# A 2048-wide hybrid diffusion layer on one core: both early z pieces of a modulation step placed behind all four conditioning batches of the next step

## The chip, the cores and the metric

One core of one Trainium2 chip. The metric is the time on the device in microseconds (us) of one execution; the kernel before takes 2322.63 us (median of three runs). PE is the matrix engine, ACT the scalar engine, DVE the vector engine, POOL the GpSimd engine, SP the engine whose queue issues the weight loads here.

## The reference

One layer of a diffusion backbone for 128 context tokens and 256 latent tokens (384 columns in all), in float32. Only its opening matters here: a conditioning vector gives a shift and a scale for every one of the 2048 channels, the normalised tokens are modulated with them, and the result is multiplied by the wide input projection.

```python
mod = (jax.nn.silu(cond) @ w_ada + b_ada)[:, None, :]
sh1, sc1, g1, sh2, sc2, g2 = jnp.split(mod, N_MOD, axis=-1)
h = rmsnorm(x, norm_mix_pre) * (1 + sc1) + sh1
z = h @ w_in + b_in
```

The three mixer branches, the output projection and the feed-forward part follow; the change does not touch them.

## The kernel before, in words

All weights pass through one list, `stream`, of pieces. Each piece has a load, for most a split, and a use. `run_stream` walks the list; SP issues the loads in the order of the list, as far ahead as there are buffers: 8 buffers `eraw` of 1 MB for the conditioning batches, 4 buffers `raw` of at most 512 KB for all other weights. A load whose buffer is still in use holds up the loads behind it. At most 8 loads are under way at once, since each takes one of eight semaphores in turn.

Float32 products are made from three matmuls (`mm3`, lines 177 to 179) on a high and a low half. So an ordinary weight piece is split first: ACT writes the high half `whi` (line 168), DVE the low half `wlo` (line 169). The split of a piece is issued two matmul pieces ahead of its use. A conditioning batch is not split (`whole`).

The first 150 us work on the scale `S1` and the shift `H1` in eight modulation steps, g = 0 to 7. Step g has four **conditioning batches** ada(g, 0) to ada(g, 3) of 1 MB each (line 393, 4 matmuls of 128x512 with 32 weight columns; the trace counts each of them twice). When the fourth is through, `ada_rows` copies the sums to the tile `row` (ACT, line 401), `ada_cols` turns them into columns with 4 very small matmuls (PE, line 410; "the turn" below), and `ada_mod` computes `S1` and `H1` of two channel tiles (DVE, lines 417 to 419) and then the modulated inputs `hx` of channel tiles 2g and 2g+1: DVE line 366, ACT lines 370, 371 and 374, DVE line 378.

With these two `hx` tiles, seven column tiles of z get two of their sixteen contributions at once, from two **early z pieces**: z(g, 0) with four column tiles (512 KB, 24 matmuls of 128x384) and z(g, 1) with three (384 KB, 18 matmuls). z(0) to z(6) stand in the loop over g, among the batches of the next step; z(7) comes later. Behind the loop stand two pieces of a further column tile, `TY`, with 8 and 6 contributions.

The functions of a piece's `after` run behind the use of the next piece, and one waiting background function of each of three queues behind that:

```python
pc.use(*his.pop(j))          # line 258
...
for f in pend:
    f()                      # ada_rows of the piece before: copy, queue ada_cols
pend = list(pc.after)        # line 265
for b in bgq:
    if b:
        b.popleft()()        # ada_cols at once, ada_mod one piece later
```

So what the list holds just behind ada(g, 3) decides where PE meets the turn, and what it holds behind that decides where `ada_mod` stands on DVE and ACT. Each engine works through its instructions in order.

In the list before, step g (from 1 on) reads ada(g, 0), ada(g, 1), ada(g, 2), z(g-1, 0), ada(g, 3), z(g-1, 1). The copy of `row` is issued behind z(g-1, 1), the turn right behind it, `ada_mod` behind ada(g+1, 0).

## Time and profile before

| | |
|---|---|
| median of three runs | 2322.63 us (2322.43 to 2324.74) |
| the profiled execution | 2323.49 us |
| its span, first to last instruction | 2321.7 us |
| PE busy | 2265.5 us, 98% |
| DVE busy | 1426.9 us, 61% |
| ACT busy | 881.0 us, 38% |
| mean granted PE clock | 0.992 |
| bytes read from HBM | 382.71 MB |

In the views below a row of the timeline has the start and the length of a run of equal instructions, their engine, line and tiles, and in brackets the idle time before them with what ended it. A row of a table of windows gives, for the stretch at its start, its length, the busy time of PE, PE's weight loads (PEld), DVE, ACT and POOL with their instructions, the granted PE clock (1.00 is full), the busy share of the DMA engines and the GB/s they moved.

### The profile page before, as it was taken

To read this page: it belongs to the slowest core of one execution; us is meant where nothing else is said; L and a number is where in the kernel's file an instruction comes from. 1 tells how busy PE (TensorE), PEld (TensorE's weight loads), DVE (VectorE), ACT (ScalarE), POOL (GpSimd) and SP (SyncE) were. 2 spreads that over 40 slices of the span, in tenths; PEclk is the share of its full clock that TensorE was granted. 3 is DMA by queue.
4 is the path that set the end of the run, shared out by engine and by line. 5 is a ranking of instruction groups with operands and counts; after the bars stand their busy time and mean duration, and the time that the engine had idled before them with its cause. 6 is when DMAs were issued, how large, how long until landed. Compare 5 with 4: busy or idle time off the path is not lost.

```text
span 2321.7 us, 31781 instructions
## 1 busy us (share of the span) xinstructions
PE 2265.5 (98%) x12597; PEld 2150.1 (93%) x12597; DVE 1426.9 (61%) x2230; ACT 881.0 (38%) x1362; POOL 31.7 (1%) x72
## 2 busy tenths in 40 slices
PE   6899999999999999999999999999999999999997
PEld 3679999999999999999989999999999999888886
DVE  3247777656788888878556577776444445444444
ACT  3243333444323323324356533333333334334333
POOL 0000000000000000000000000000000000000000
PEclk9999999999999999999999999999999999999999
DMA  9825333234666666768533355554343333344343
GB/s 398 350 97 148 105 117 120 96 120 154 200 227 224 223 222 228 234 197 289 183 97 121 130 189 181 188 185 162 127 140 124 128 123 124 132 130 145 127 131 105
DMA packets 104869, 390.05 MB, mean 168 GB/s; under 512 B 12112, under 2 KB 12256, under 8 KB 100624
## 3 DMA queue, kind: packets, MB, share of 16 engines
q1 hardware_dynamic: 99504, 371.76, 47.5%
q0 software_dynamic: 4064, 14.36, 2.0%
q8 instruction: 98, 1.61, 0.3%
q10 hardware_dynamic: 1152, 1.90, 0.2%
q14 instruction: 51, 0.42, 0.1%
HBM read 382.71 MB, written 5.27 MB: 167 GB/s over the span
## 4 chain that ended last, share of the span: by engine, by line
PE 92%; DVE 1%; ACT 0%; issue 0%; DVEq 0%; ACTq 0%
PE ps L179 23%; PE ps L177 23%; PE ps L178 23%; PE ps L1490 5%; PE ps L1491 5%; PE ps L1489 5%; PE ps L877 1%; PE ps L878 1%; PE ps L876 1%; PE ps L973 1%; PE ps L968 1%; PE ps L912 0%; DVE wlo L169 0%; PE ps L921 0%; PE ps L1013 0%; PE ps L1033 0%
## 5 line engine op out<-in xcount | busy, mean ns | idle before, releaser
L169 DVE TENSOR_TENSOR wlo<-raw,whi 128x1024 fp32r<-128x1024 f32 (+3 forms) x521 | 622.0, 1197 | 725.5 <-ACT whi L168 725.0
L177 PE MATMUL ps<-hx,whi 128*128 128x384 f32 (+1 forms) x3024 | 1028.2, 340 | 19.1 <-ACT whi L168 13.4
L179 PE MATMUL ps<-hx,wlo 128*128 128x384 f32 (+1 forms) x3024 | 1022.9, 338 | 4.4 <-DVE wlo L169 4.4
L178 PE MATMUL ps<-hx,whi 128*128 128x384 f32 (+1 forms) x3024 | 1022.0, 338 | 0.3 <-DVE hx L169 0.2
L168 ACT ACTIVATE whi<-raw 128x1024 fp32r<-128x1024 f32 (+3 forms) x521 | 540.0, 1038 | 1234.2 <-PE ps L178 741.9
L177 PEld LDWEIGHTS ps<-hx,whi 128*128 128x128 f32 x3024 | 572.5, 189 | 33.2 <-ACT whi L168 19.6
L179 PEld LDWEIGHTS ps<-hx,wlo 128*128 128x128 f32 x3024 | 572.4, 189 | 7.0 <-DVE wlo L169 7.0
L178 PEld LDWEIGHTS ps<-hx,whi 128*128 128x128 f32 x3024 | 572.5, 189 | 1.9 <-DVE hx L378 0.7
L1154 DVE SCALAR_TENSOR_TENSOR cb<-raw,cb 128x1024 f32<-128x1024 f32 x256 | 313.0, 1223 | 10.0 <-DMA raw<-w_ada 4.0
L1490 PE MATMUL ps<-whi,hx 128*128 128x512 f32 x528 | 205.5, 389 | 0.8 <-DVE hx L169 0.8
L1489 PE MATMUL ps<-whi,hx 128*128 128x512 f32 x528 | 205.5, 389 | 0.0
L1491 PE MATMUL ps<-wlo,hx 128*128 128x512 f32 x528 | 205.4, 389 | 0.0
L1490 PEld LDWEIGHTS ps<-whi,hx 128*128 128x128 f32 x528 | 99.1, 188 | 21.8 <-DVE hx L169 1.1
L1489 PEld LDWEIGHTS ps<-whi,hx 128*128 128x128 f32 x528 | 99.1, 188 | 20.8 <-ACT hx L168 0.4
L1491 PEld LDWEIGHTS ps<-wlo,hx 128*128 128x128 f32 x528 | 99.1, 188 | 20.5
L691 DVE SCALAR_TENSOR_TENSOR cacc<-cbuf,vec,cacc 128x444 f32<-128x444 f32 x116 | 78.7, 678 | 2.8
L1381 DVE SCALAR_TENSOR_TENSOR t<-t,vec,t 128x192 f32<-128x192 f32 (+1 forms) x176 | 63.7, 383 | 16.0 <-ACT t L1372 12.8
L876 PE MATMUL ps<-whi,hx 128*128 128x256 f32 x192 | 56.5, 294 | 0.0
L393 PE MATMUL ps<-eraw,cs 128*32 128x512 f32 x256 | 37.3, 697 | 17.4 <-DMA eraw<-w_ada 16.7
L877 PE MATMUL ps<-whi,hx 128*128 128x256 f32 x192 | 54.3, 283 | 0.0
L878 PE MATMUL ps<-wlo,hx 128*128 128x256 f32 x192 | 54.3, 283 | 0.0
L169 DVE TENSOR_TENSOR hx<-f,hx 128x384 fp32r<-128x384 f32 x88 | 48.3, 550 | 0.0
(283 smaller groups left out, 1430.0 us busy)
## 6 DMA issues: line engine op xcount, KB each, us to landing
raw<-w_up SPq DMA_DIRECT2D x164, 512.0 KB, 3.7
raw<-w_in SPq DMA_DIRECT2D x163, 512.0 KB, 3.8
raw<-w_ada SPq DMA_DIRECT2D x128, 512.0 KB, 4.4
raw<-w_down SPq DMA_DIRECT2D x88, 512.0 KB, 3.3
eraw<-w_ada SPq DMA_DIRECT2D x32, 1024.0 KB, 14.1
raw<-w_out SPq DMA_DIRECT2D x32, 512.0 KB, 4.5
raw<-w_v SPq DMA_DIRECT2D x16, 512.0 KB, 4.0
raw<-w_br SPq DMA_DIRECT2D x16, 512.0 KB, 5.0
```

The source lines that it names most:

```text
L168: act.activation(hi, src, AF.Copy)
L169: dve.tensor_sub(lo, src, hi.bitcast(F32))
L177: pe.matmul(out, wh, x, start=first, stop=False, skip_group_check=True)
L178: pe.matmul(out, wh, xl, start=False, stop=False, skip_group_check=True)
L179: pe.matmul(out, wl, x, start=False, stop=last, skip_group_check=True)
L691: dve.scalar_tensor_tensor(a, b[:, j : j + CPOS], w, a, ALU.mult, ALU.add)
L876: pe.matmul(outs[t], xh, hi[:, a], start=k == 0 and t != 1, stop=False, skip_group_check=True)
L877: pe.matmul(outs[t], xl, hi[:, a], start=False, stop=False, skip_group_check=True)
L1154: dve.scalar_tensor_tensor(MX["junk"], raw, 1.0, MX["cb"][c][half], ALU.mult, ALU.mult, accum_out=MODR[:, m, n, c, half : half + 1])
L1489: pe.matmul(ps, xh, hi[:, w], start=first, stop=False, skip_group_check=True)
L1490: pe.matmul(ps, xl, hi[:, w], start=False, stop=False, skip_group_check=True)
L1491: pe.matmul(ps, xh, lo[:, w], start=False, stop=last, skip_group_check=True)
```

## The change

Both early z pieces leave their places among the batches and go behind the fourth one. Step g now reads ada(g, 0), ada(g, 1), ada(g, 2), ada(g, 3), z(g-1, 0), z(g-1, 1). The same instructions are issued, as many as before; loads, splits and matmuls follow the list in its new order.

```diff
             stream.append(Piece(i["w_ada1"][g, :, 4 * q : 4 * q + 4], (4, 512), ada_use(g, q), early=True, whole=True,
                                 after=[ada_rows(g)] if q == 3 else None,
                                 onload=load_all_x if g == 0 and q == 0 else None))
-            if q > 1 and g:
-                stream.append(early_piece(g - 1, q - 2))
+        if g:
+            stream.append(early_piece(g - 1, 0))
+            stream.append(early_piece(g - 1, 1))
     stream.append(part_piece(TY, 7, 0, 8))
     stream.append(part_piece(TY, 7, 8, 14))
```

PE, the end of z(0, 0) in step 1 and what follows it, before (L177 to L179 are z, L393 a conditioning batch, L410 the turn):

```order
L179 MATMUL ps_106<-hx_255,wlo_233 128x384
L393 MATMUL ps_214<-eraw_134,cs 32x512 x4
L177 MATMUL ps_107<-hx_251,whi_267 128x384
L178 MATMUL ps_107<-hx_251,whi_267 128x384
L179 MATMUL ps_107<-hx_251,wlo_268 128x384
```

The same place in the change:

```order
L179 MATMUL ps_106<-hx_251,wlo_256 128x384
L410 MATMUL ps_103<-pair,row_303 128x2 x4
L177 MATMUL ps_107<-hx_247,whi_265 128x384
L178 MATMUL ps_107<-hx_247,whi_265 128x384
L179 MATMUL ps_107<-hx_247,wlo_266 128x384
```

The fourth batch is gone from between the two z pieces, and the turn of step 1 stands there instead.

PE, from the end of z(0, 1) to the first matmuls of z(1, 0), before:

```order
L179 MATMUL ps_109<-hx_255,wlo_268 128x384
L410 MATMUL ps_103<-pair,row_321 128x2 x4
L393 MATMUL ps_327<-eraw_143,cs 32x512 x4
L393 MATMUL ps_327<-eraw_160,cs 32x512 x4
L393 MATMUL ps_327<-eraw_178,cs 32x512 x4
L177 MATMUL ps_103<-hx_343,whi_351 128x384
```

And in the change:

```order
L179 MATMUL ps_109<-hx_251,wlo_266 128x384
L393 MATMUL ps_344<-eraw_143,cs 32x512 x4
L393 MATMUL ps_344<-eraw_160,cs 32x512 x4
L393 MATMUL ps_344<-eraw_178,cs 32x512 x4
L393 MATMUL ps_344<-eraw_196,cs 32x512 x4
L177 MATMUL ps_103<-hx_336,whi_357 128x384
```

Between the turn and z(1, 0) there were three batches; now there are z(0, 1) and four batches.

DVE, the opening, from the reciprocal of the token scale on, before (S and H are `S1` and `H1`):

```order
L346 RECIPROCAL r_226<-t_224 128x384
L169 TENSOR_TENSOR wlo_233<-raw_132,whi_232 128x1024
L417 SCALAR_TENSOR_TENSOR S_76<-ps_103,vec 128x4
L418 TENSOR_TENSOR S_76<-S_76,vec 128x4
L419 TENSOR_TENSOR H_77<-ps_103,vec 128x4
L366 TENSOR_TENSOR t_245<-x_94,r_226 128x384
L366 TENSOR_TENSOR t_247<-x_94,r_226 128x384
L378 TENSOR_TENSOR hx_251<-t_245,hx_251 128x384
L378 TENSOR_TENSOR hx_255<-t_247,hx_255 128x384
L169 TENSOR_TENSOR wlo_268<-raw_136,whi_267 128x768
```

And in the change:

```order
L346 RECIPROCAL r_226<-t_224 128x384
L417 SCALAR_TENSOR_TENSOR S_76<-ps_103,vec 128x4
L418 TENSOR_TENSOR S_76<-S_76,vec 128x4
L419 TENSOR_TENSOR H_77<-ps_103,vec 128x4
L366 TENSOR_TENSOR t_241<-x_94,r_226 128x384
L366 TENSOR_TENSOR t_243<-x_94,r_226 128x384
L378 TENSOR_TENSOR hx_247<-t_241,hx_247 128x384
L378 TENSOR_TENSOR hx_251<-t_243,hx_251 128x384
L169 TENSOR_TENSOR wlo_256<-raw_134,whi_255 128x1024
L169 TENSOR_TENSOR wlo_266<-raw_136,whi_265 128x768
```

The split of z(0, 0) now stands behind the modulation of step 0; before it stood ahead of it. ACT's order moves in the same way there. From step 1 on, DVE and ACT keep their order before and after: `ada_mod`, then the splits of z(g, 0) and z(g, 1).

## The prediction

> **What bounds the kernel now.** I read the page first, then a table of windows over the opening and the rest, then the timelines of PE, ACT and DVE over one modulation step.

> ```profile
> span 2321.7 us, 31781 instructions
> PE 2265.5 (98%) x12597; PEld 2150.1 (93%) x12597; DVE 1426.9 (61%) x2230; ACT 881.0 (38%) x1362; POOL 31.7 (1%) x72
> 52.83:69.67 16.84, 13.97 (x82) 10.44 (x82) 4.53 (x10) 5.18 (x10) 0.00 (x0) 0.90 1.01 414
> 69.67:86.61 16.94, 14.08 (x83) 10.54 (x83) 4.55 (x10) 5.19 (x10) 0.00 (x0) 0.90 0.97 378
> 86.61:103.61 17.00, 14.13 (x82) 10.61 (x83) 4.53 (x10) 5.18 (x10) 0.00 (x0) 0.90 0.79 302
> 103.61:120.61 17.00, 14.13 (x83) 10.60 (x83) 4.54 (x10) 5.19 (x10) 0.00 (x0) 0.90 0.62 246
> 120.61:137.61 17.00, 14.14 (x83) 10.61 (x83) 4.53 (x10) 5.18 (x10) 0.49 (x1) 0.90 0.15 54
> 137.61:149.53 11.92, 11.28 (x59) 9.87 (x59) 4.16 (x4) 3.85 (x5) 2.91 (x6) 0.86 0.44 145
> 150.00:2322.00 2172.00, 2152.72 (x11980) 2072.62 (x11978) 1381.59 (x2146) 830.48 (x1275) 25.78 (x57) 1.00 0.48 158
> ```

> PE is busy 98% of the span, and behind 150 us it is busy for 2152.72 of 2172.00 us. What moves the start of that stretch moves the end of the kernel. The changed code lies ahead of it. There every step, from the first matmul of one z(g, 0) to that of the next, takes 16.84 to 17.00 us, whether the loads run at 414 GB/s or at 54 GB/s: the step does not wait for memory. PE is busy 14.1 us of the 17.0, with a clock of 0.90. So two things are lost in each step: idle time and clock.

> One step on PE (x8 and x24 are one and three conditioning batches):

> ```profile
> 59.53 1.06 PE L393 MATMUL ps<-eraw,cs 128*32 128x512 f32 x8
> 60.53 0.45 PE L177 MATMUL ps<-hx,whi 128*128 128x384 f32 x1
> ...
> 63.78 0.95 PE L410 MATMUL ps<-pair,row 128*128 128x2 f32 x8
> 64.66 2.78 PE L393 MATMUL ps<-eraw,cs 128*32 128x512 f32 x24
> 69.67 0.45 PE L177 MATMUL ps<-hx,whi 128*128 128x384 f32 x1 [2.23 <-ACT whi L168]
> ...
> 70.93 0.69 PE L179 MATMUL ps<-hx,wlo 128*128 128x384 f32 x1 [0.64 <-DVE wlo L169]
> ```

> A batch alone takes 1.00 us from start to start (59.53 to 60.53), z(g, 1) 3.25 us for 18 matmuls (60.53 to 63.78), the turn 0.88, three batches 2.78. Then PE stands 2.23 us for `whi`, and 0.64 us for `wlo` two matmuls later.

> What it waits for starts with the turn, on DVE and ACT (DVE's rows first):

> ```profile
> 64.77 0.16 DVE L417 SCALAR_TENSOR_TENSOR S<-ps,vec 128x4 f32<-128x4 f32 x1 [9.87 <-PE ps L410]
> ...
> 65.12 1.01 DVE L366 TENSOR_TENSOR t<-x,r 128x384 f32<-128x384 f32 x2
> 65.70 0.49 ACT L370 ACTIVATE t<-t,H,S 128x128 f32<-128x128 f32 x1 [4.44 <-DVE t L366]
> ...
> 68.58 1.77 ACT L168 ACTIVATE whi<-raw 128x1024 fp32r<-128x1024 f32 x2
> PE ps L177 <- ACT whi L168: 13.4, 6, 2.2
> PE ps L179 <- DVE wlo L169: 3.8, 6, 0.6
> ```

> The turn ends at 64.66. DVE makes `S1` at 64.77, the products at 65.12; ACT makes the two `hx` from 65.70 to 68.58, and only then splits z(g, 0). From the end of the turn to the first matmul it is 69.67 - 64.66 = 5.01 us, to the first use of `wlo` 70.93 - 64.66 = 6.27 us. Three batches cover 2.78 us of this. The two waits come six times, 13.4 and 3.8 us in total.

> The clock is lost for the same reason:

> ```profile
> 84.40:87.90 3.50, 0.65 (x3) 0.33 (x3) 2.24 (x4) 2.86 (x5) 0.00 (x0) 1.00 0.95 386
> 87.90:91.30 3.40, 3.40 (x11) 3.40 (x12) 0.78 (x1) 0.00 (x0) 0.00 (x0) 0.51 1.01 426
> ...
> 98.10:101.40 3.30, 3.28 (x30) 1.16 (x29) 1.52 (x6) 1.73 (x4) 0.00 (x0) 1.00 0.73 226
> 101.40:104.90 3.50, 0.65 (x3) 0.33 (x3) 2.24 (x4) 2.86 (x5) 0.00 (x0) 1.00 0.94 393
> 104.90:108.30 3.40, 3.40 (x11) 3.40 (x12) 0.78 (x1) 0.00 (x0) 0.00 (x0) 0.51 1.00 422
> ```

> In the stretch that holds the waits (84.40 to 87.90) PE is busy 0.65 us of 3.50; in the 3.40 us behind it the granted clock is 0.51, and full again after that. The same again at 101.40. The cold stretch does 1.67 us of work less than a warm one (3.40 x 0.49). [...]

> **The change part by part.** No instruction is added or removed. Three things move.

> *The turn goes ahead of z(g, 1), and the fourth batch ahead of the next z.* The chain of 5.01 us (6.27 for `wlo`) then runs beside z(g, 1), 3.25 us, and four batches, 2.78 + 0.93 = 3.71: 6.96 us in all. The first matmul has 1.9 us to spare. The first `wlo` use, some 0.3 us later, has 1.0. Both waits go. The copy of `row` that the turn needs runs on ACT beside z(g, 0), which takes 24/18 x 3.25 = 4.33 us, so the turn does not wait. With no stretch of low PE activity I expect the clock to stay full: the window 98.10 to 101.40 is nearly all batches, and the one behind it has 1.00, so batches count as activity; the turn alone is 0.88 us.

> A step is then 4.33 (z, first piece) + 0.88 + 3.25 + 3.71 = 12.17 us. In the trace z(1, 0) to z(6, 0) are five steps, 16.84 + 16.94 + 3 x 17.00 = 84.78 us by the windows above. Five new ones are 60.85. **Gain 23.9 us.**

> *The tail.* From the start of z(6, 0) to the first `TY` matmul the trace has 11.92 us, with a batch, a `wlo` wait and a cold stretch in it. Now z(6, 0), the turn and z(6, 1): 4.33 + 0.88 + 3.25 = 8.46. **Gain 3.5 us.** The last `hx` pair has z(6, 1) and both `TY` pieces as cover, more than before.

> *The opening.* DVE (three rows) and PE (the last) there:

> ```profile
> 29.32 2.55 DVE L346 RECIPROCAL r<-t 128x384 f32<-128x384 f32 x1 [12.12 <-ACT t L344]
> 32.33 1.23 DVE L169 TENSOR_TENSOR wlo<-raw,whi 128x1024 fp32r<-128x1024 f32 x1 [0.46 <-ACT whi L168]
> 33.47 0.15 DVE L417 SCALAR_TENSOR_TENSOR S<-ps,vec 128x4 f32<-128x4 f32 x1
> 36.05 0.45 PE L177 MATMUL ps<-hx,whi 128*128 128x384 f32 x1 [2.45 <-ACT hx L374]
> ```

> Before, `wlo` of z(0, 0) went ahead of `S1`. Now `S1` starts at 29.32 + 2.55 = 31.87. The chain of the other steps from there (69.67 - 64.77 = 4.90, 70.93 - 64.77 = 6.16) puts the first z matmul at 36.8 and the first `wlo` use at 38.0. Before it was 36.05 without a `wlo` wait: about 1.0 us later now. Against that stand the 2.23 us wait of z(1, 0), which goes, and the batches, now 3.71 behind z(0, 1) for 1.00 + 2.78: z(1, 0) starts 2.3 - 1.0 = 1.3 us earlier. The clock is cold here and could stay so one window longer (1.7 us), or catch up 0.6. **Gain 1.3 us, between -0.4 and 1.9.**

> *SP's queue.* Loads follow the list, so each step's two z loads go behind its fourth batch. A step loads 4 batches and 512 + 384 KB, 5.11 MB:

> ```profile
> 0.00:15.00 15.00, 0.00 (x0) 0.00 (x0) 6.85 (x15) 8.69 (x18) 2.52 (x8) 1.00 0.89 342
> 15.00:75.00 60.00, 49.25 (x247) 29.13 (x248) 18.06 (x32) 17.64 (x30) 0.00 (x0) 0.91 1.01 417
> 75.00:90.00 15.00, 12.14 (x76) 8.61 (x76) 4.54 (x9) 5.18 (x9) 0.00 (x0) 0.93 0.96 374
> eraw<-w_ada SPq DMA_DIRECT2D x32, 1024.0 KB, 14.1
> SPq L205 <- PE ps L393: 44.3, 17, 6.4
> ```

> At the 417 GB/s of 15 to 75 us this is 12.26 us, just over PE's 12.17. So after the change PE and the loads go at about the same pace, and the lead decides. Up to ada(7, 3) the queue brings 3.46 MB of inputs (2048 x 384 tokens and a 128 x 615 vector tile in float32), 32 x 1.049 MB and six pairs of z, 42.5 MB. By 15 us 5.13 MB are there (342 GB/s), the rest takes 37.4 / 0.417 = 89.7 us: ada(7, 3) lands at 104.7. PE reaches it at z(6, 0) less 0.9 us. By my times z(1, 0) starts near 51.5, z(6, 0) near 112.4, so the load is 6.8 us ahead. The first lead, ada(2, 3) landed at 43.4 for a use at 50.6, is 7.2. The loads' buffers come free soon enough: ada(5, 3) is used near 88, and ada(7, 0) has to be under way by about 95. The later fall in rate is no limit of memory: 302 GB/s x 17.00 us is 5.13 MB, exactly one step, at the pace at which PE frees buffers (SP's 44.3 us of waits for L393). I cost the loads at nothing; their cover is this lead.

> Sum: 23.9 + 3.5 + 1.3 = 28.7 us. The profiled execution took 2323.49 us for a span of 2321.7, which lies 0.86 above the median. I put the gain against the median: 2322.63 - 28.7 = **2293.9 us**. Bounds of this case: with the opening at its ends and 0.1 us of hand-over per step either way, 2290 to 2297.

> **The rivals.**

> *The cold stretch stays.* If these short gaps are not what cools the clock, it is something else in the step, the batches with their 32 columns or the turn, and these stay. Then each of six z(g, 0) keeps its 1.67 us, 10 us in all: 2304. Against it: every cold stretch here follows a window with 0.65 us of work, and windows full of batches are followed by a full clock. [...]

> *The loads do not keep their pace.* At the 374 GB/s of 75 to 90 us instead of 417, ada(7, 3) lands at 15 + 37.4 / 0.374 = 115 us, 3.6 us too late: 2297.5. A rate near this would come if a buffer were freed late in every step. Against it: SP has 8 loads under way and the batches are used 7 us behind their landing.

> *Slower.* The z pieces now need the whole 5.11 MB of a step ahead of them, and everything behind the loop waits for z(6). If the loads fell to the 246 GB/s of 103.61 to 120.61 from the beginning, ada(7, 3) would land at 15 + 37.4 / 0.246 = 167 us, `TY` would start at 167 + 0.9 + 8.5 = 176.4 instead of 149.53, and the time would be 2349.5. The point from which this decides is a landing at 140, that is 299 GB/s. The 417 GB/s of the opening speak against it.

> *The gain is given back later*, since the `raw` loads of the stretch behind 150 us have to come 29 us earlier: 2322. Against it: 54 GB/s at 120 to 137 us show an empty queue, four `raw` buffers ahead.

> **How the numbers follow.** My forecast has 0.74, the cold stretch 0.12, the slower loads 0.08, given back 0.03, slower 0.03. The first alone spans 2290 to 2297. The range of 8 in 10 goes to 2304.5, as far as the cold stretch, and to 2289.5 below: PE could do a step in a little less, but not below its matmuls. A measurement of this kernel can tell about 0.2% (4.6 us) from no change. Faster: 0.94; same: 0.03; slower: 0.03.

> **What would show it.** In the profile of the changed kernel the waits of L177 for `whi` and of L179 for `wlo` ahead of 120 us are down to the opening's; the PE clock between 45 and 120 us is 1.00; the first matmuls of z(g, 0) are 12.2 us apart; `TY` starts near 121 us; the loads run at over 400 GB/s up to 105 us; the stretch behind it is as long as before, some 2172 us. I am wrong if PE waits for `eraw` behind 45 us (the lead was too small), if the clock still shows 0.5 once in a step, or if the stretch behind `TY` has grown.

## The result, and the profile after

The changed kernel takes 2294.22 us (median of four runs, 2293.20 to 2294.96) against 2322.95 us before: the ratio is 0.9871, with a 95% interval of 0.986 to 0.9883. That is 28.7 us less. A second set of runs of the same kernel gave 2293.71 us and 0.9868 (0.9854 to 0.9883).

The same table of windows as for before, on the changed kernel: five steps from z(1, 0) to z(6, 0), the tail up to the first `TY` matmul, and the rest.

```profile
52.17:64.14 11.97, 11.97 (x87) 9.09 (x83) 4.54 (x10) 5.20 (x9) 0.00 (x0) 1.00 1.01 413
...
76.11:88.08 11.97, 11.97 (x87) 9.09 (x83) 4.54 (x10) 5.20 (x9) 0.00 (x0) 1.00 1.01 415
...
100.04:112.01 11.97, 11.97 (x87) 9.09 (x83) 4.54 (x10) 5.97 (x10) 0.49 (x1) 1.00 0.83 336
112.01:120.23 8.22, 8.22 (x54) 8.22 (x51) 3.70 (x8) 2.83 (x6) 2.91 (x6) 1.00 0.57 189
120.23:2293.20 2172.97, 2153.97 (x11983) 2073.89 (x11981) 1380.47 (x2141) 830.30 (x1274) 25.77 (x57) 1.00 0.48 158
```

A step takes 11.97 us instead of 17.00, PE is busy for all of it, and the clock is 1.00 instead of 0.90. Loads run at 413 to 419 GB/s up to 100 us. What follows `TY` is as long as before, 2173 us.

The timeline of PE in the changed kernel, from the first z matmul to that of the next step:

```profile
36.85 0.69 PE L177 MATMUL ps<-hx,whi 128*128 128x384 f32 x1 [2.38 <-ACT whi L168]
...
38.11 0.69 PE L179 MATMUL ps<-hx,wlo 128*128 128x384 f32 x1 [0.25 <-DVE wlo L169]
...
43.40 0.36 PE L177 MATMUL ps<-hx,whi 128*128 128x384 f32 x1
...
44.48 0.95 PE L410 MATMUL ps<-pair,row 128*128 128x2 f32 x8
45.30 0.42 PE L177 MATMUL ps<-hx,whi 128*128 128x384 f32 x1
...
48.59 3.64 PE L393 MATMUL ps<-eraw,cs 128*32 128x512 f32 x32
52.17 0.44 PE L177 MATMUL ps<-hx,whi 128*128 128x384 f32 x1
```

Who PE waited for between 30 and 140 us (us in total, times, longest):

```profile
PE ps L177 <- ACT whi L168: 2.4, 1, 2.4
PE ps L179 <- DVE wlo L169: 0.2, 1, 0.2
```

The turn stands between z(0, 0) and z(0, 1), four batches run in 3.64 us, and z(1, 0) starts with no idle time before it. The waits for `whi` and `wlo`, 13.4 and 3.8 us before, are 2.4 and 0.2 us, both in the opening.

### The profile page after: what moved, and what is told of

Read it like the earlier page. It is cut to its first block, busy times and chain, and to the rows that moved or that the text cites. A ratio compares the mean times of both kernels' runs of the same rounds, so it can differ in the third digit from the quotient of the medians.

```text
span 2293.2 us, 31786 instructions
## 1 busy us (share of the span) xinstructions
PE 2253.0 (98%) x12597; PEld 2143.6 (93%) x12597; DVE 1426.8 (62%) x2230; ACT 880.8 (38%) x1362; POOL 31.7 (1%) x72
## 4 chain that ended last, share of the span: by engine, by line
PE 97%; DVE 1%; DMA 1%; ACT 1%; issue 0%; ACTq 0%; DVEq 0%
PE ps L177 24%; PE ps L179 24%; PE ps L178 24%; PE ps L1491 5%; PE ps L1490 5%; PE ps L1492 5%; PE ps L393 1%; PE ps L878 1%; PE ps L879 1%; PE ps L877 1%; DMA eraw<-w_ada 1%; PE ps L974 1%; PE ps L969 1%; PE ps L913 0%; DVE wlo L169 0%; DMA vec<-vec 0%
## 5 line engine op out<-in xcount | busy, mean ns | idle before, releaser
L169 DVE TENSOR_TENSOR wlo<-raw,whi 128x1024 fp32r<-128x1024 f32 (+3 forms) x521 | 622.2, 1197 | 726.9 <-ACT whi L168 724.7
L177 PE MATMUL ps<-hx,whi 128*128 128x384 f32 (+1 forms) x3024 | 1024.8, 339 | 5.6 <-ACT hx L1294 3.2
L179 PE MATMUL ps<-hx,wlo 128*128 128x384 f32 (+1 forms) x3024 | 1019.1, 337 | 0.8 <-DVE wlo L169 0.8
L168 ACT ACTIVATE whi<-raw 128x1024 fp32r<-128x1024 f32 (+3 forms) x521 | 540.0, 1038 | 1231.8 <-PE ps L178 748.2
L177 PEld LDWEIGHTS ps<-hx,whi 128*128 128x128 f32 x3024 | 570.4, 189 | 12.3 <-issue 5.0
L179 PEld LDWEIGHTS ps<-hx,wlo 128*128 128x128 f32 x3024 | 570.1, 189 | 2.0 <-DVE wlo L169 2.0
L393 PE MATMUL ps<-eraw,cs 128*32 128x512 f32 x256 | 34.7, 675 | 18.6 <-DMA eraw<-w_ada 18.6
L169 DVE TENSOR_TENSOR hx<-f,hx 128x384 fp32r<-128x384 f32 x88 | 48.3, 550 | 0.0
## 6 DMA issues: line engine op xcount, KB each, us to landing
eraw<-w_ada SPq DMA_DIRECT2D x32, 1024.0 KB, 17.1
```

What stands on the lines that cost most here:

```text
L168: act.activation(hi, src, AF.Copy)
L169: dve.tensor_sub(lo, src, hi.bitcast(F32))
L177: pe.matmul(out, wh, x, start=first, stop=False, skip_group_check=True)
L179: pe.matmul(out, wl, x, start=False, stop=last, skip_group_check=True)
```

## The experiments

My theory: the chain behind the turn (S1, products, hx, split) set the step; the change covers it with z(g, 1) and one more batch, which takes the idle time away and with it the cold clock behind it. Rivals: the four batches in one run and the new order of loads bring the gain; the batches themselves cool the clock; the loads are the near bound.

**Only the turn moved.** The list stays as before; copy and turn are issued inside the use of ada(g, 3).

```diff
 # in ada_use, behind the four matmuls
+            if q == 3 and g:
+                ada_rows(g)()
+                bgq[1].pop()()
 # the batch in the loop
-                                after=[ada_rows(g)] if q == 3 else None,
+                                after=[ada_rows(g)] if q == 3 and g == 0 else None,
```

> The list of before (loads, batches and z pieces in their old order); only the copy of row and the turn are issued right behind ada(g, 3), ahead of z(g-1, 1), from step 1 on. My theory, the chain behind the turn sets the step: z(g-1, 1) and three batches, 3.25 + 2.78 = 6.03 us, cover the 5.01 us to the first matmul, so the waits for whi and wlo go and the clock stays at 1.00; instead PE waits some 0.85 us per step for the copy of row. Step 4.33 + 1.00 + 0.85 + 0.88 + 3.25 + 2.78 = 13.1 us, time about 2300.6 (2298 to 2304). Rival A, what gains is the four batches in one run and the loads in the new order: this kernel keeps most of the 17.0 us step, over 2313. Rival B, batches or the turn cool the clock: the waits go, but a clock of about 0.5 for 3.4 us stays in each step, about 2311.

Measured: 2302.57 us against 2323.78 beside it, ratio 0.991 (0.9895 to 0.9924). PE's waits from 30 to 150 us in this kernel:

```profile
PE ps L413 <- ACT row L404: 5.0, 7, 0.7
PE ps L177 <- ACT hx L374: 2.4, 1, 2.4
```

Two turns in its timeline of PE (L413 is the turn there):

```profile
57.67 1.05 PE L413 MATMUL ps<-pair,row 128*128 128x2 f32 x8 [0.72 <-ACT row L404]
...
70.75 1.05 PE L413 MATMUL ps<-pair,row 128*128 128x2 f32 x8 [0.72 <-ACT row L404]
```

The waits for the split are gone, the new one for the copy is 0.72 us, a step is 70.75 - 57.67 = 13.08 us (13.1 expected) and the clock from 45 to 120 us is 1.00. So 21 of the 29 us come from the turn's place alone, with loads and batches in their old order. Rivals A and B fall.

**Only the turn left behind.** The list of the change, with the copy and the turn behind z(g-1, 1).

```diff
-                                after=[ada_rows(g)] if q == 3 else None,
+                                after=[ada_rows(g)] if q == 3 and g == 0 else None,
 ...
-            stream.append(early_piece(g - 1, 0))
+            stream.append(early_piece(g - 1, 0, after=[ada_rows(g)]))
```

> The list of the change; only the copy of row and the turn are issued one piece later, behind z(g-1, 1) as before. My theory: four batches cover 3.71 of the 5.01 us, so PE waits 1.3 us for whi and about 0.6 for wlo in each of six steps, 11.6 us in all: 2306 if the clock stays full with about 1.5 us of work in a window of 3.4, 2316 if that still halves it. Rival A, the order of loads and batches alone brings the gain: 2294 to 2296.

Measured: 2309.24 us, ratio 0.9936 (0.9921 to 0.9951), 15 us more than the change. One step's two waits in its timeline of PE:

```profile
65.92 0.44 PE L177 MATMUL ps<-hx,whi 128*128 128x384 f32 x1 [1.37 <-ACT whi L168]
...
67.17 0.45 PE L179 MATMUL ps<-hx,wlo 128*128 128x384 f32 x1 [0.64 <-DVE wlo L169]
```

A table of windows of 3.41 us, on the grid on which the one cold stretch of these steps begins and ends (the first three around the step above, the last two around the next):

```profile
61.94:65.35 3.41, 2.61 (x28) 0.52 (x16) 1.39 (x3) 3.34 (x7) 0.00 (x0) 1.00 1.02 416
65.35:68.76 3.41, 2.20 (x11) 1.88 (x12) 2.25 (x3) 1.73 (x3) 0.00 (x0) 1.00 1.00 411
68.76:72.17 3.41, 3.41 (x22) 3.41 (x21) 0.00 (x0) 0.00 (x0) 0.00 (x0) 1.00 1.04 420
79.00:82.41 3.41, 1.67 (x8) 1.35 (x9) 2.65 (x3) 2.27 (x4) 0.00 (x0) 1.00 0.98 399
82.41:85.82 3.41, 3.41 (x13) 3.41 (x12) 0.00 (x0) 0.00 (x0) 0.00 (x0) 0.50 1.04 425
```

Both steps have the same waits, 1.37 and 0.64 us (1.36 in the second). Waits of 1.3 and 0.6 us were expected. The time lies between the two given, 2306 with a full and 2316 with a halved clock: the profiled execution has one cold stretch in six steps. In the first step shown the waits fall into two windows with 2.61 and 2.20 us of work, and the clock stays full. In the second step they leave one window with 1.67 us of work, and the clock behind it is 0.50. In the sixth step the same waits leave one window with 1.90 us of work, and the clock behind it stays full:

```profile
123.40:126.82 3.42, 1.90 (x9) 1.58 (x10) 3.03 (x4) 2.51 (x3) 2.51 (x6) 1.00 0.25 41
126.82:130.23 3.41, 3.41 (x22) 3.41 (x21) 0.67 (x1) 0.74 (x1) 0.00 (x0) 1.00 0.94 320
```

Of these four windows only the one with the least work, 1.67 us, was followed by half clock. In the kernel before the clock changes on such a grid, too: its half-clock stretches in the steps begin at 53.80, 70.87, 87.93, 105.00, 122.07 and 139.13 us, 17.07 us apart, which is five times 3.41. The first three in its table of windows:

```profile
53.80:57.21 3.41, 3.12 (x10) 3.13 (x11) 1.10 (x2) 0.00 (x0) 0.00 (x0) 0.50 1.03 416
...
70.87:74.28 3.41, 3.35 (x10) 3.35 (x11) 0.87 (x2) 0.00 (x0) 0.00 (x0) 0.50 1.02 422
...
87.93:91.35 3.42, 3.42 (x11) 3.42 (x12) 0.75 (x1) 0.00 (x0) 0.00 (x0) 0.50 1.01 426
```

Its step of 17.00 us is almost five windows long, so the gap meets nearly the same place of the grid in every step.

**The gap filled with useless work.** The kernel before, with 20 small matmuls behind the third batch of steps 2 to 7.

```diff
+            if q == 2 and g > 1:
+                for n in range(20):
+                    pe.matmul(acc["z", EARLY[1 + n % 6]][:, NT:512], hx[0].hi[:, :P], hx[0].lo[:, :P], start=False,
+                              stop=False, skip_group_check=True)
```

> The kernel before, with 20 small matmuls of 128x128 added behind the third batch of each step from 2 on, in the gap in which PE waits for whi; their sums go into columns that nobody reads. They change no wait, only PE's activity in the gap. My theory, the gap cools the clock: the clock behind it stays at 1.00, z(g, 0) is 1.67 us shorter in six steps, time 2322.9 - 10 = 2313 (2311 to 2316). [...]

Measured: 2316.49 us, ratio 0.9967 (0.9956 to 0.9979), 7.3 us less than the 2323.78 of before beside it and 0.5 above my range. One step in its timeline of PE (L397 is the small matmuls):

```profile
64.08 2.78 PE L393 MATMUL ps<-eraw,cs 128*32 128x512 f32 x24
66.79 2.45 PE L397 MATMUL ps<-hx 128*128 128x128 f32 x20
69.09 0.44 PE L177 MATMUL ps<-hx,whi 128*128 128x384 f32 x1
...
70.35 0.45 PE L179 MATMUL ps<-hx,wlo 128*128 128x384 f32 x1 [0.64 <-DVE wlo L169]
```

The window that follows this gap, in its table of windows:

```profile
69.40:72.80 3.40, 2.76 (x16) 2.45 (x15) 1.76 (x2) 0.38 (x1) 0.00 (x0) 1.00 1.04 424
```

The small matmuls fill the gap up to 69.09, 5.01 us behind the end of the turn at 64.08, as before; no wait has become shorter but `whi`'s, which is now work. The clock behind is 1.00, and the step 15.4 us (turns at 63.20 and 78.64) for 17.0. In all six steps of this execution the clock behind the gap is full, 1.00 for 0.50 in the kernel before. So the gap was what cooled the clock: six steps shortened by some 1.5 us are 9 us. Of these 0.8 were lost in the opening, whose turn of step 1 came at 47.78 us for 46.94 before. By the last turn 8.4 us are gained (140.36 for 148.72), but the whole span is only 6.9 us shorter. Far behind the changed steps, at 1181 us, the clock is half for 10.2 us, where the kernel before has 6.8 us of it at 1190 us; 3.4 us more at half clock take back about 1.7 us.

**Four buffers for batches instead of eight**, once in the change and once in the kernel before (`ERAW` 8 to 4).

> The change with 4 instead of 8 buffers for batches: the load of ada(g+1, q) can then only start when ada(g, q) is used, so the lead of some 7 us that I named as the cover of the loads is taken away. My theory of the lead: four batches freed within 3.6 us need 10.1 us to load and some 2 us to start, the two z loads stand behind them, so z(g, 0) comes up to 1.2 us late: step 12.0 to 13.2 us, time 2294 to 2302, likeliest 2298, with PE waits for whi, wlo or eraw in each step. Rival, the loads are the near bound of the step: each step goes to 15 us or more, over 2312.

> The kernel before with 4 instead of 8 buffers for batches. My theory: its 17.0 us step is set by the chain behind the turn and needs 5.11 MB in 17.0 us, 301 GB/s, so the lost lead costs it little: 2322 to 2327, against some 9 us for the change with 4 buffers. Rival, lead matters as much to the old order: over 2330.

Measured: the change 2303.56 us (2299.41 to 2305.23), ratio 0.9916 (0.9899 to 0.9933); the kernel before 2324.79 us, ratio 1.0002 (0.9992 to 1.0011). PE's waits from 30 to 150 us with four buffers in the change:

```profile
PE ps L177 <- ACT whi L168: 5.7, 4, 2.5
PE ps L179 <- DVE wlo L169: 3.2, 5, 0.6
```

ACT's wait for loads there, from 40 to 122 us:

```profile
ACT whi L168 <- DMA raw<-w_in: 12.3, 7, 3.2
```

The lead does matter to the change (about 10 us) and not to the old order. My likeliest value, 2298, was too low by 5.6, and the median lies above my range for this run; what comes late is not a batch but the `raw` tile of a z piece, for which ACT waits. The 2 us put down for the start of a load were my estimate; in the kernel before, 512 KB that are under way alone land 3.2 us after their issue at 151.09 us, and at 417 GB/s their bytes take 1.26 of these. In the old order with four buffers, as with the turn left behind, the same waits do not halve the clock every time. Two of its steps, from turn to turn, with the same waits of 2.23 and 0.65 us, and below them, for each, the clock's window that holds the waits and the one behind it:

```profile
82.21:97.63 15.42, 12.54 (x84) 9.02 (x84) 4.54 (x9) 5.19 (x9) 0.00 (x0) 1.00 0.86 330
65.22:82.21 16.99, 14.11 (x84) 10.59 (x84) 4.54 (x9) 5.19 (x9) 0.00 (x0) 0.90 0.81 303
...
87.20:90.61 3.41, 1.87 (x9) 1.55 (x10) 2.58 (x3) 1.58 (x2) 0.00 (x0) 1.00 1.01 425
90.61:94.03 3.42, 3.42 (x25) 2.67 (x23) 0.00 (x0) 0.00 (x0) 0.00 (x0) 1.00 0.99 414
...
70.14:73.55 3.41, 1.79 (x9) 1.48 (x10) 2.65 (x3) 1.65 (x2) 0.00 (x0) 1.00 0.99 375
73.55:76.96 3.41, 3.41 (x12) 3.41 (x11) 0.00 (x0) 0.00 (x0) 0.00 (x0) 0.50 0.97 387
```

The second step is cold for a fifth of its time and takes 16.99 us, the first stays warm and takes 15.42. A window with 1.87 us of work left the clock full, one with 1.79 us was followed by half clock.

**A shorter opening.** The change, with the token norm's end one piece earlier; and the same with one full matmul more behind ada(1, 3).

```diff
-    for c in range(4):
-        bgq[0].append(lambda c=c: rms1_part(c))
+    bgq[0].append(lambda: (rms1_part(0), rms1_part(1)))
+    bgq[0].append(lambda: rms1_part(2))
+    bgq[0].append(lambda: rms1_part(3))
     bgq[0].append(rms1_end)
 # second kernel, in ada_use
+            if q == 3 and g == 1:
+                pe.matmul(acc["z", EARLY[1]][:, :NT], ones, R["ss1"], start=True, stop=True, skip_group_check=True)
```

> The change itself once more, as the measure for the two kernels beside it. Every theory: 2294 (2293 to 2295), 0.987 of before.

> The change, with two of the four parts of the sum of squares issued behind the first batch, so that the end of the token norm (one matmul, root, reciprocal) is issued behind ada(0, 3) and not behind ada(1, 0). In the profile of the change S1 of step 0 waits for the reciprocal, which ends at 31.9 us; PE sits idle between the batches from 15 to 25 us. My theory: what is left to gain lies in the opening, on the chain norm, S1, hx, whi, first z matmul at 36.85. The reciprocal ends near 29.4, the turn at 29.6, S1 starts 2.2 us earlier, the first z matmul near 34.7, all behind it 2 us earlier: about 2292, 0.9862 of before. Rival: the load of z(0, 0) or the cold clock sets the start of z: 2294 as the change.

> As the kernel with the early norm, and one more full matmul (ones by the sum of squares, into a bank that z(0, 0) clears) behind ada(1, 3), in the gap in which PE waits for the first hx. In the profile of the change z(0, 0) runs cold up to 43.4 us, 7 us behind its start. My theory, a window with little work cools the clock: the filler keeps a window busy, the clock comes back up to 3.4 us earlier, up to 1.7 us gained: 2290.5 to 2292. Rival: the clock needs a full warm window of z matmuls anyhow: as without the filler, or 0.5 to 1 us later where it overruns the gap.

Measured: 2293.55 us, ratio 0.9868 (0.9853 to 0.9883), and 2293.27 us, 0.9866 (0.9849 to 0.9882), beside 2293.71 us of the change: no difference that can be told. The first of the two, the first z matmul and three turns in its timeline of PE:

```profile
34.97 0.44 PE L177 MATMUL ps<-hx,whi 128*128 128x384 f32 x1 [1.30 <-ACT whi L168]
...
65.87 0.95 PE L410 MATMUL ps<-pair,row 128*128 128x2 f32 x8
...
78.45 0.95 PE L410 MATMUL ps<-pair,row 128*128 128x2 f32 x8
...
90.67 0.95 PE L410 MATMUL ps<-pair,row 128*128 128x2 f32 x8
```

ACT's wait for loads in it, from 40 to 122 us:

```profile
ACT whi L168 <- DMA raw<-w_in: 6.7, 7, 1.4
```

The split of z(3, 0) and z(3, 1) in its timeline of ACT:

```profile
72.14 1.85 ACT L168 ACTIVATE whi<-raw 128x1024 fp32r<-128x1024 f32 x2 [1.37 <-DMA raw<-w_in]
```

And the same in the timeline of ACT in the change, with the split of z(6, 0) and z(6, 1) below:

```profile
73.22 1.77 ACT L168 ACTIVATE whi<-raw 128x1024 fp32r<-128x1024 f32 x2
...
109.12 1.77 ACT L168 ACTIVATE whi<-raw 128x1024 fp32r<-128x1024 f32 x2
```

The opening did become shorter: the first z matmul starts at 34.97 us (36.67 in the change's run beside it), the turn of step 1 at 41.63 (44.04). But the two steps shown then take 12.58 and 12.22 us, and the six from the first turn to the last 12.25 us on average. That is the pace of the loads (12.26 us at 417 GB/s), and ACT waits seven times for `raw`. By the last turn only 0.7 us of the 2.4 is left (115.14 for 115.84). With the full matmul more the cold stretch of the opening ended earlier, at 38.5 us for 39.4, and the turn of step 1 came at 41.24, but the loads took that back too. That the added matmul ended it earlier is not shown: in that execution the clock's windows begin 0.95 us earlier on the grid, and its cold stretch is the longer one, 31.66 to 38.48 us for 36.02 to 39.43. My theory of the opening was right, my time for it wrong; the rival was right on the time, though by the loads of the later z pieces more than by that of z(0, 0). In the change the split of z(3, 0) starts at 73.22 without a wait; here it starts at 72.14, when its load has landed. In the change that load is issued at 56.0 us and lands 16.2 us later, at 72.2, so the change has one microsecond to spare there. For z(6, 0) it has only 0.2 us: the load lands at 108.9, and the split starts at 109.12.

## Why the prediction was right, step by step

- *The step.* 12.17 us forecast, 11.97 measured; most of the difference lies in the four batches, which take 3.57 us in one run (60.56 to 64.13) and not 3.71. Five steps and their start: z(1, 0) at 52.17 to z(6, 0) at 112.01, 59.84 us for 84.78 before: 24.9 us gained, 23.9 forecast. The parts are shown apart: the cover of the chain by the run with the turn left behind (waits of 1.37 and 0.64 us come back), the clock by the filler.
- *The clock.* The rival that the cold stretch stays did not come: 1.00 in every step, with four batches in a run. The filler shows the short gaps as the cause: with the chain of 5.01 us as long as before and only the gap filled, the clock stays at 1.00.
- *The tail.* 8.22 us for 11.92: 3.7 us gained, 3.5 forecast.
- *The opening.* The first z matmul was put at 36.8 and came at 36.85, the first `wlo` use 38.0 and 38.11. But the clock stayed cold up to 43.40, the window longer that I had allowed for, so z(1, 0) came 0.7 us earlier (52.17 for 52.83) and not 1.3. I had priced that window at 1.7 us; z(0, 0) took 1.0 us longer than before (7.63 for 6.64). Why the clock stayed low for a second window there is not shown.
- *The loads.* Cost nothing, as forecast, and the rate held at 413 to 419 GB/s. But the cover was mis-sized. By bytes and rate I put ada(2, 3) and ada(7, 3) 7.2 and 6.8 us ahead of their use; in the trace they land at 46.2 and 107.6 us, about 5.0 and 3.5 us ahead. And I took the batches' lead alone and left out the z loads, which land last in each step and must still be split. By bytes z(3, 0) should have landed at 15 + (27.7 - 5.13) / 0.417 = 69 us (27.7 MB are its place in the queue); it landed at 72.2, 1.0 us ahead of its split. As a step of 11.97 us is shorter than the 12.26 us of its loads, this margin shrinks from step to step, down to 0.2 us at z(6, 0). So the rival of the slower loads was nearer than I had it. With four buffers, and with a shorter opening, this is what set the time.
- *Later.* 2173.0 us behind `TY` for 2172.2 before: only 0.8 us was given back. The sum 0.7 + 24.9 + 3.7 - 0.8 is 28.5, the difference of the two spans.
- *The number.* That 28.7 us were forecast and the medians differ by 28.7 is luck to the last digit: the opening and the stretch behind `TY` gave 0.6 and 0.8 us less than forecast, the steps and the tail 1.0 and 0.2 us more. The bounds of the forecast, 2290 to 2297, are also wider than their terms: the opening between -0.4 and 1.9 us and 0.1 us in each of six steps give 2292.7 to 2296.2.

## What to carry to other kernels

Where an engine waits at the same place in every step, follow the chain back to the instruction that starts it, here four tiny matmuls, and move that start ahead of work that does not need it; the turn's place alone gave 21 of 29 us with no other order changed. Look at the granted clock behind a gap on PE as well as at the gap: in the kernel before, the matmuls behind gaps of 2.23 and 0.64 us ran at half clock for 3.41 us, which cost some 1.7 us more in each step. Once the chain is covered, ask which transfer lands last before its use with its preparation included, not the largest one: that margin says whether the next improvement will be seen.

## What the runs showed of the hardware

So two steps of the same instructions, in one execution of the old order with four buffers, took 15.42 us at a granted clock of 1.00 and 16.99 us at 0.90. Twenty matmuls of 128x128 in a step, 2.3 us of work that nobody reads, kept the clock at 1.00 there and made the kernel 7.3 us faster.
